# Average pooling of 8,192 rows: 15,304 neighbouring cells and 1,080 of the rest per partition, the rest loaded in two halves

## The chip, the cores and the metric

The kernel runs on one core of a Trainium2 chip. The metric is device time in microseconds of one execution; the number for a kernel is the median of several runs. A profile shows one execution from its first to its last instruction, the span; the time of a run is somewhat longer than the span.

## The reference

The input `x` is 32 x 256 x 4,096 in float32, that is 8,192 rows of 4,096 numbers (134.2 MB). Each row is cut into 256 windows of 16 neighbours, and each output cell is the mean of one window. The output is 32 x 256 x 256 in float32 (8.4 MB).

```python
for i in range(output_size):
    start = int(i * length / output_size)
    end = int((i + 1) * length / output_size)
    result[:, :, i] = np.mean(x[:, :, start:end], axis=-1)
```

Windows don't cross rows and rows lie one after the other, so in memory the whole task is 2,097,152 windows of 16 numbers in a line, each giving one cell. Where the line is cut among the 128 partitions is free.

## The kernel before, in words

The 128 partitions share the rows. The first 7,680 rows are the part called "many": partition p owns rows 60p to 60p + 59 (983,040 bytes of `x`, 15,360 cells). The other 512 rows are the part called "last": partition p owns four of them (65,536 bytes, 1,024 cells).

The loop over `t` (line 62) makes 16 tiles. In each, every partition gets four rows, 16,384 numbers: tiles 0 to 14 come from "many", tile 15 is "last". A tile lies in a buffer `xin` from a pool of two buffers (line 64), so tile t + 2 can be loaded only when the work on tile t has read its buffer for the last time. The last tile is put 32 numbers (128 bytes) into its buffer (line 65).

Per tile there are five steps.
- Line 75: SP issues the load, one DMA of 128 partitions x 65,536 bytes. At t = 1 a small memset on DVE (line 74) goes ahead of it into the same buffer, so that the load waits for it.
- Line 78: POOL adds, for the second half of the cells (512), the upper eight numbers of each window to the lower eight, in place.
- Line 83: DVE sums all 16 numbers of each window for the first half of the cells.
- Line 86: DVE sums the remaining eight numbers of each window for the second half. It waits for POOL and is the last to read the buffer.
- Line 89: ACT multiplies the 1,024 sums by 1/16, in place. The results stay in SBUF: `res_many` for tiles 0 to 14, `res_last` for tile 15.

There are three stores, all issued on SP like the loads. The one of `res_many` (7.9 MB, line 77, issued through the helper at line 58) stands in the program right behind the load of tile 15, and waits for ACT on tile 14. After the loop `res_last` is stored in two DMAs of 120 and of 8 partitions (line 95), which wait for ACT on tile 15. The program ends when all three stores have counted up the semaphore `stored` (line 100).

The order on each engine is the order of the program. The waits between engines and DMAs come from the tile framework, which tracks who writes and reads what.

Of the kernel before, what the change touches and what calls it, by code (L numbers as in the profile page):

```python
# [1 line left out]

# [4 lines left out]


@with_exitstack
def kernel(  # L10
    ctx: ExitStack,
    tc: tile.TileContext,
    x: bass.AP,
    output_size: int,
    out: bass.AP,
):

    nc = tc.nc
    F32 = mybir.dt.float32
    X = mybir.AxisListType.X

    batch, channels, length = x.shape
    ob, oc, olen = out.shape
    assert ob == batch and oc == channels and olen == output_size
    assert length % output_size == 0
    window = length // output_size  # L30
    hw = window // 2
    inv_w = 1.0 / float(window)

    P = nc.NUM_PARTITIONS
    R = 4
    rows = batch * channels
    assert rows % (P * R) == 0
    ntiles = rows // (P * R)
    many = (ntiles - 1) * R
    cells = R * output_size  # L40
    m = cells // 2
    cols = R * length

    xr = x.rearrange("b c l -> (b c) l")
    orow = out.rearrange("b c o -> (b c) o")
    x_many = xr[0 : P * many, :].rearrange("(p r) l -> p (r l)", p=P, r=many)
    o_many = orow[0 : P * many, :].rearrange("(p r) o -> p (r o)", p=P, r=many)
    x_last = xr[P * many :, :].rearrange("(p r) l -> p (r l)", p=P, r=R)
    o_last = orow[P * many :, :].rearrange("(p r) o -> p (r o)", p=P, r=R)

    res_many = nc.alloc_sbuf_tensor("res_many", [P, (ntiles - 1) * cells], F32, align_bytes=256)
    res_last = nc.alloc_sbuf_tensor("res_last", [P, cells], F32, align_bytes=256)
    inpool = ctx.enter_context(tc.tile_pool(name="inpool", bufs=2))

    stored = nc.alloc_semaphore("stored")

    def store(out, in_):
        ins = nc.sync.dma_start(out=out, in_=in_)
        tc.no_tile_sem_insts.add(ins.ins.name)
        ins.then_inc(stored, 16)  # L60

    for t in range(ntiles):
        last = t == ntiles - 1
        xbuf = inpool.tile([P, cols + 64], F32, name="xin")
        off = 32 if last else 0
        flat = xbuf[:, off : off + cols]
        xin = flat.rearrange("p (o w) -> p o w", w=window)
        if last:
            res, base, src = res_last, 0, x_last
        else:  # L70
            res, base = res_many, t * cells
            src = x_many[:, t * cols : (t + 1) * cols]
        if t == 1:
            nc.vector.memset(flat[:, 0:1536], 0.0)  # L74
        nc.sync.dma_start(out=flat, in_=src)
        if last:
            store(o_many, res_many[:, :])
        nc.gpsimd.tensor_add(  # L78
            out=xin[:, m:cells, 0:hw],
            in0=xin[:, m:cells, 0:hw],  # L80
            in1=xin[:, m:cells, hw:window],
        )
        nc.vector.reduce_sum(  # L83
            out=res[:, base : base + m], in_=xin[:, 0:m, :], axis=X
        )
        nc.vector.reduce_sum(  # L86
            out=res[:, base + m : base + cells], in_=xin[:, m:cells, 0:hw], axis=X
        )
        nc.scalar.mul(  # L89
            out=res[:, base : base + cells],  # L90
            in_=res[:, base : base + cells],
            mul=inv_w,
        )
    for lo, hi in ((0, 120), (120, P)):
        store(o_last[lo:hi, :], res_last[lo:hi, :])

    ctx.pop_all().close()
    tc.close()
    tc.compile()  # L99
    nc.sync.wait_ge(stored, 48)  # L100
    nc.sync.sem_clear(stored)


# [1 line left out]
_INS = ['x', 'output_size']  # L105
_OUTS = [((32, 256, 256), 'float32')]

_NUMBERS = {'output_size': 256}


# [26 lines left out]
```

## Time and profile before

| what | value |
|---|---|
| median of 3 runs | 333.42 us (333.3 to 333.7) |
| span of the profiled execution | 332.3 us |
| time around the span (median less span) | 1.1 us |
| DVE busy | 211.0 us (64%) |
| POOL busy | 139.7 us (42%) |
| ACT busy | 18.2 us (5%) |
| DMA packets | 2,599 with 142.61 MB, 99.4% of 16 engines' span |
| read from and written to DRAM | 134.22 MB and 8.39 MB, 429 GB/s over the span |

The profile gives busy times per engine, a picture of the span in 40 equal slices (a digit is the busy share in tenths), groups of instructions by line, the waits, and the chain of waits that ended last. The profiled execution has no other time of its own than its span; the median of the runs stands beside it. SPq is SP's queue of DMA issues. A DMA of this kernel moves one packet per partition, and 16 DMA engines share the packets; each engine ends its part of a DMA with a packet of 4 bytes that counts up a semaphore. The trace keeps a start, a duration and a size for every packet.

### The profile page before, as it was taken

What the parts mean: (1) busy time and instruction counts of PE and PEld (TensorE: products, weight loads), DVE (VectorE), ACT (ScalarE), POOL (GpSimd) and SP (SyncE); (2) the same over time, 40 slices, a digit from 0 to 9 for tenths busy, and PEclk for the clock granted to TensorE, in tenths of its full rate; (3) what the DMA queues carried; (4) which work ended last, traced back from release to release, by engine and by line L of the source; (5) the groups of instructions that cost most, each with busy time, mean ns of one, the idle gap of its engine ahead of it and who ended that gap; (6) DMA issues with size and microseconds to landing.
All of it is one profiled execution on the core that took longest, in us unless ns stands there. A gap on an engine that the chain in (4) does not pass through costs nothing.

```text
span 332.3 us, 162 instructions
## 1 busy us (share of the span) xinstructions
DVE 211.0 (64%) x33; ACT 18.2 (5%) x17; POOL 139.7 (42%) x20
## 2 busy tenths in 40 slices
DVE  1029396692939669392956939295683929578392
ACT  1000101001010100001010000101000010101001
POOL 0027091642709164370906437090633709063370
DMA  9898999989898999989898998989899898989897
GB/s 379 379 505 379 489 394 442 442 379 505 379 505 379 489 394 394 489 379 505 379 497 387 426 458 379 505 379 505 379 481 402 387 497 379 505 379 505 363 473 300
DMA packets 2599, 142.61 MB, mean 429 GB/s; under 512 B 295, under 2 KB 295, under 8 KB 423
## 3 DMA queue, kind: packets, MB, share of 16 engines
q1 hardware_dynamic: 2599, 142.61, 99.4%
HBM read 134.22 MB, written 8.39 MB: 429 GB/s over the span
## 4 chain that ended last, share of the span: by engine, by line
DMA 65%; POOL 18%; DVE 11%; POOLq 3%; issue 0%; ACT 0%
DMA xin<-in_x_dram 65%; POOL xin L78 18%; DVE res_many L86 9%; POOLq L99 3%; DVE res_last L86 1%; DVE xin L74 0%; ACT res_last L89 0%; POOLq L78 0%
## 5 line engine op out<-in xcount | busy, mean ns | idle before, releaser
L78 POOL TENSOR_TENSOR xin<-xin 128x4096 f32<-128x4096 f32 x16 | 139.5, 8717 | 181.9 <-DMA xin<-in_x_dram 181.9
L83 DVE TENSOR_REDUCE res_many<-xin 128x512 f32<-128x8192 f32 x15 | 130.3, 8686 | 105.0 <-DMA xin<-in_x_dram 105.0
L86 DVE TENSOR_REDUCE res_many<-xin 128x512 f32<-128x4096 f32 x15 | 66.3, 4420 | 2.4 <-POOL xin L78 2.3
L89 ACT ACTIVATE res_many<-res_many 128x1024 f32<-128x1024 f32 x15 | 15.8, 1056 | 289.7 <-DVE res_many L86 289.7
L83 DVE TENSOR_REDUCE res_last<-xin 128x512 f32<-128x8192 f32 x1 | 8.7, 8686 | 6.6 <-DMA xin<-in_x_dram 6.6
L86 DVE TENSOR_REDUCE res_last<-xin 128x512 f32<-128x4096 f32 x1 | 4.4, 4422 | 0.2 <-POOL xin L78 0.2
L89 ACT ACTIVATE res_last<-res_last 128x1024 f32<-128x1024 f32 x1 | 1.1, 1056 | 18.8 <-DVE res_last L86 18.8
L74 DVE MEMSET xin<- 128x1536 f32 x1 | 1.3, 1338 | 1.1 <-PEq L118 1.1
L89 ACT ACT_TABLE_LOAD x1 | 1.3, 1283 | 0.7 <-PEq L118 0.7
L118 POOL MEMSET const-float32-0.0<- 128x1 f32 x1 | 0.1, 98 | 0.2 <-issue 0.2
L118 POOL MEMSET const-bfloat16-1.0<- 128x1 bf16 x1 | 0.1, 101 | 0.0
L118 POOL MEMSET const-uint8-127<- 128x1 uint8 x1 | 0.1, 101 | 0.0
L118 POOL MEMSET const-float32-1.0<- 128x1 f32 x1 | 0.1, 98 | 0.0
## 6 DMA issues: line engine op xcount, KB each, us to landing
out_dram<-res_many SPq DMA_DIRECT2D x1, 7680.0 KB
out_dram<-res_last SPq DMA_DIRECT2D x1, 480.0 KB
xin<-in_x_dram SPq DMA_DIRECT2D x16, 25.3
out_dram<-res_last SPq DMA_DIRECT2D x1, 32.0 KB
```

The lines of the kernel that those rows point to most:

```text
L74: nc.vector.memset(flat[:, 0:1536], 0.0)
L78: nc.gpsimd.tensor_add(out=xin[:, m:cells, 0:hw], in0=xin[:, m:cells, 0:hw], in1=xin[:, m:cells, hw:window],)
L83: nc.vector.reduce_sum(out=res[:, base : base + m], in_=xin[:, 0:m, :], axis=X)
L86: nc.vector.reduce_sum(out=res[:, base + m : base + cells], in_=xin[:, m:cells, 0:hw], axis=X)
L89: nc.scalar.mul(out=res[:, base : base + cells], in_=res[:, base : base + cells], mul=inv_w,)
L99: tc.compile()
L118: nc = _bacc.Bacc("TRN2", target_bir_lowering=False, num_devices=1)
```

## The change

The line of 2,097,152 windows is cut elsewhere. "Many" now gives each partition 15,304 neighbouring cells (979,456 bytes of `x`, not a whole number of rows), and "last" gives each 1,080 (69,120 bytes). Fourteen tiles of "many" have 1,024 cells as before, the fifteenth has 968. The buffers hold 1,080 cells, and the last tile is no longer put 128 bytes into its buffer. "Last" is loaded into one buffer by two DMAs of 540 cells per partition, both issued ahead of the store of `res_many`; POOL, DVE and ACT then work on each half by itself (270 cells by the one way, 270 by the other). The stores are three as before, of 61,216 bytes per partition for `res_many` and 4,320 for `res_last`, the latter in 120 and 8 partitions.

```diff
-    R = 4
-    rows = batch * channels
-    ntiles = rows // (P * R)
-    many = (ntiles - 1) * R
-    cells = R * output_size
-    m = cells // 2
-    cols = R * length
...
-    x_many = xr[0 : P * many, :].rearrange("(p r) l -> p (r l)", p=P, r=many)
-    o_many = orow[0 : P * many, :].rearrange("(p r) o -> p (r o)", p=P, r=many)
...
+    N = 1024
+    windows = batch * channels * output_size
+    few = N + 56
+    many = windows // P - few
+    sizes = [N] * (many // N) + [many % N] * (many % N > 0)
+    cols = few * window
...
+    x_many = xf[0 : P * many * window].rearrange("(p n) -> p n", p=P)
+    o_many = of[0 : P * many].rearrange("(p n) -> p n", p=P)
+    x_last = xf[P * many * window :].rearrange("(p n) -> p n", p=P)
+    o_last = of[P * many :].rearrange("(p n) -> p n", p=P)
...
+    def pooled(flat, res):
+        n = res.shape[1]
+        m = n // 2
...
+    done = 0
+    for t, n in enumerate(sizes):
+        xbuf = inpool.tile([P, cols], F32, name="xin")
+        flat = xbuf[:, 0 : n * window]
         if t == 1:
             nc.vector.memset(flat[:, 0:1536], 0.0)
+        nc.sync.dma_start(
+            out=flat, in_=x_many[:, done * window : (done + n) * window]
         )
+        pooled(flat, res_many[:, done : done + n])
+        done += n
+
+    xbuf = inpool.tile([P, cols], F32, name="xin")
+    half = few // 2
+    halves = [(0, half), (half, few)]
+    for lo, hi in halves:
+        nc.sync.dma_start(
+            out=xbuf[:, lo * window : hi * window],
+            in_=x_last[:, lo * window : hi * window],
         )
+    store(o_many, res_many[:, :])
+    for lo, hi in halves:
+        pooled(xbuf[:, lo * window : hi * window], res_last[:, lo:hi])
     for lo, hi in ((0, 120), (120, P)):
         store(o_last[lo:hi, :], res_last[lo:hi, :])
```

`pooled` holds the add on POOL, the two reductions on DVE and the multiplication on ACT, as lines 78 to 93 did.

More of the change, by code (lines that the diff above doesn't have):

```diff
@@ L34 @@
     P = nc.NUM_PARTITIONS
-    R = 4
-    rows = batch * channels
-    assert rows % (P * R) == 0
-    ntiles = rows // (P * R)
-    many = (ntiles - 1) * R
-    cells = R * output_size
-    m = cells // 2
-    cols = R * length
-    xr = x.rearrange("b c l -> (b c) l")
-    orow = out.rearrange("b c o -> (b c) o")
-    x_many = xr[0 : P * many, :].rearrange("(p r) l -> p (r l)", p=P, r=many)
-    o_many = orow[0 : P * many, :].rearrange("(p r) o -> p (r o)", p=P, r=many)
[L48 to L52, printed above, removed]
+    N = 1024
+    windows = batch * channels * output_size
+    assert windows % P == 0
+    few = N + 56
+    many = windows // P - few
+    sizes = [N] * (many // N) + [many % N] * (many % N > 0)
+    cols = few * window
+    xf = x.rearrange("b c l -> (b c l)")
+    of = out.rearrange("b c o -> (b c o)")
+    x_many = xf[0 : P * many * window].rearrange("(p n) -> p n", p=P)
+    o_many = of[0 : P * many].rearrange("(p n) -> p n", p=P)
+    x_last = xf[P * many * window :].rearrange("(p n) -> p n", p=P)
+    o_last = of[P * many :].rearrange("(p n) -> p n", p=P)
+    res_many = nc.alloc_sbuf_tensor("res_many", [P, many], F32, align_bytes=256)
+    res_last = nc.alloc_sbuf_tensor("res_last", [P, few], F32, align_bytes=256)
     inpool = ctx.enter_context(tc.tile_pool(name="inpool", bufs=2))
@@ L60, in store @@
         ins.then_inc(stored, 16)
[L62 to L66, printed above, removed]
-        xin = flat.rearrange("p (o w) -> p o w", w=window)
[L68 to L72, printed above, removed]
+    def pooled(flat, res):
+        n = res.shape[1]
+        m = n // 2
+        xin = flat.rearrange("p (o w) -> p o w", w=window)
+        nc.gpsimd.tensor_add(
+            out=xin[:, m:n, 0:hw], in0=xin[:, m:n, 0:hw], in1=xin[:, m:n, hw:window]
+        )
+        nc.vector.reduce_sum(out=res[:, 0:m], in_=xin[:, 0:m, :], axis=X)
+        nc.vector.reduce_sum(out=res[:, m:n], in_=xin[:, m:n, 0:hw], axis=X)
+        nc.scalar.mul(out=res, in_=res, mul=inv_w)
@@ L73 @@
+    done = 0
+    for t, n in enumerate(sizes):
+        xbuf = inpool.tile([P, cols], F32, name="xin")
+        flat = xbuf[:, 0 : n * window]
         if t == 1:
             nc.vector.memset(flat[:, 0:1536], 0.0)
[L75 to L81, printed above, removed]
-        )
-        nc.vector.reduce_sum(
-            out=res[:, base : base + m], in_=xin[:, 0:m, :], axis=X
-        )
@@ L86 @@
[L86 to L93, printed above, removed]
+        nc.sync.dma_start(
+            out=flat, in_=x_many[:, done * window : (done + n) * window]
+        )
+        pooled(flat, res_many[:, done : done + n])
+        done += n
+    xbuf = inpool.tile([P, cols], F32, name="xin")
```

## The prediction

> **What bounds the kernel now.** I read the page's parts 2 and 3 first (is an engine full?), then the chain of waits (does one piece of work end last?), then the timeline of the end, then the packet records that the trace keeps for its DMA engines, one start, duration and size per packet.
>
> From the page:
> ```profile
> span 332.3 us, 162 instructions
> ...
> DVE  1029396692939669392956939295683929578392
> ...
> POOL 0027091642709164370906437090633709063370
> DMA  9898999989898999989898998989899898989897
> ...
> DMA packets 2599, 142.61 MB, mean 429 GB/s; under 512 B 295, under 2 KB 295, under 8 KB 423
> ...
> q1 hardware_dynamic: 2599, 142.61, 99.4%
> ```
> The DMA row is at 8 or 9 tenths in every slice but the last, and its packets fill 99.4% of 16 engines' span, while DVE and POOL have gaps all along. So the time is the bytes, 142.61 MB, at the engines' pace.
>
> The chain of waits seems to say something else:
> ```profile
> 273.94 8.73 POOL xin L78
> 282.67 0.02 issue
> 282.69 4.43 DVE res_many L86
> 287.12 0.02 issue
> 287.14 25.86 DMA xin<-in_x_dram
> ```
> It gives POOL 18% and DVE 11%, because it follows a load back to the reduction that freed its buffer. But the 25.86 us of that load hold a wait behind another one: load t+1 was still running when load t+2 was issued. Loads land 19.32 us apart in steady state (254.55, 273.83, 293.16 are the starts of the reductions that wait for them), so the load of 287.14 stood some 6 us in the queue. A shorter compute step would only lengthen that wait.
>
> The timeline of the end:
> ```profile
> 302.02 4.42 DVE L86 TENSOR_REDUCE res_many<-xin 128x512 f32<-128x4096 f32 x1 [0.17 <-POOL xin L78]
> 306.47 1.06 ACT L89 ACTIVATE res_many<-res_many 128x1024 f32<-128x1024 f32 x1 [18.27 <-DVE res_many L86]
> 307.55 0.35 SPq L58 DMA_DIRECT2D out_dram<-res_many  x1
> 313.02 8.69 DVE L83 TENSOR_REDUCE res_last<-xin 128x512 f32<-128x8192 f32 x1 [6.59 <-DMA xin<-in_x_dram]
> 313.13 8.72 POOL L78 TENSOR_TENSOR xin<-xin 128x4096 f32<-128x4096 f32 x1 [11.15 <-DMA xin<-in_x_dram]
> 321.88 4.42 DVE L86 TENSOR_REDUCE res_last<-xin 128x512 f32<-128x4096 f32 x1 [0.17 <-POOL xin L78]
> 326.34 1.06 ACT L89 ACTIVATE res_last<-res_last 128x1024 f32<-128x1024 f32 x1 [18.81 <-DVE res_last L86]
> 327.42 0.75 SPq L58 DMA_DIRECT2D out_dram<-res_last  x2
> ```
> The large store is issued at 307.55, before the last load has landed (313.02), and the last tile is computed while that store runs. The packet records settle whether its cover is long enough. The first packet starts at 1.76 us, 1.02 after its issue (0.74). The large store's packets start at 312.05 to 312.64, each where a load packet ended, and end at 330.2 to 330.8; the small stores' packets follow without a gap until 331.86. Chaining packets by end and next start, I find no gap over 0.06 us on any of the 16 engines. The last tile's store, issued at 327.42, could have started near 328.4 and its turn came at 330.2: the tail of compute is hidden by about 1.8 us.
>
> **A price per packet.** Median start to next start on one engine: 2,414 ns for 65,536 B, 2,264 for 61,440, 155 for 4,096. A line through the outer two is 4.4 ns + 0.03677 ns per byte; it gives 2,263 for the middle one. The 4-byte semaphore packets that end a DMA take 6. The busiest engine before: 16 loads x (8 x 2,414 + 6) = 309.09; large store 8 x 2,264 + 6 = 18.12; small stores 9 x 155 + 12 = 1.41 (120 rows on 15 engines and 8 on 8, which the 295 small packets = 17 x 16 + 15 + 8 fit); sum 328.61 us. To this come 1.76 before the first packet, 0.64 because each engine's first packet is slow (mean 3,056 against 2,418 busy), 0.35 because the last load packet of each engine, just ahead of the store, is slow too (mean 2,766), and 0.14 of small excesses between (2,201 ns over 16 engines): 331.50. Recorded: 331.86 on the last one, and 0.43 more to the end of the span at 332.29. The median of the runs, 333.42, lies 1.13 above the span; I carry that over unchanged.
>
> **The change, part by part.**
> - Loads. 14 of 65,536 B per partition: 14 x 19.318 = 270.45. One of 61,952: 8 x 2,282 + 6 = 18.26. Two halves of 34,560: 2 x (8 x 1,275 + 6) = 20.41. Stores: 61,216 B, 8 x 2,255 + 6 = 18.05; 4,320 B, 9 x 163 + 12 = 1.48. Sum 328.66, which is 0.05 us more: eight packet overheads and one semaphore packet. The bytes are the same.
> - One more DMA on SP: 0.33 us of issue (the L75 row), right after the first half's, at about 287.5. Queued behind it on SP are only the stores, the first due near 305.6. Hidden.
> - Tile 14 has 968 cells: its load ends 8 x 132 ns = 1.06 us sooner, its sum and reductions shrink by 968/1024 (8.72 to 8.24, 4.42 to 4.18), and the large store can be issued at about 292.1 + 0.1 + 8.24 + 0.1 + 4.18 + 1.0 = 305.7 instead of 307.55. Worth nothing: its packets can't start before the loads are through, near 312.1.
> - The halves take the buffer of tile 13, which is free at 287.12 as before. Tile 14's packets last until about 291.7, and packets of a DMA issued at 287.14 can start near 288.2: 3.5 us of slack (4.6 before), so the queue doesn't run dry.
> - The compute on the halves. Half 1 lands near 302.9; DVE is on tile 14 until 304.7. Half 2 lands near 313.1 and then costs 270/512 of the rows above: 4.60 on POOL, 2.33 for the second reduction, some 0.6 on ACT. The last store is issued near 320.9, not 327.42: 6.5 us earlier on paper, none of it on the path, since its packets queue behind the large store until about 330.2 either way. Were both halves to wait for the second, the reductions would sum to what they are now.
> - Layout in DRAM. A partition's rows start 979,456 B apart, not 983,040; both are multiples of 256 B. Not so in the output: 61,216 = 239 x 256 + 32 and 4,320 = 16 x 256 + 224, so seven rows of eight start off a 256 B boundary, where all started on one. No row shows a store like that. Low end: the last tile was loaded to an SBUF address 128 B off (line 65), and each engine's first seven packets of it were at 2,418 as ever: cost 0. High end: the nearest row of packets that do run slow at full load is the 0.35 us one above, 348 of 2,418 or 14%; on seven eighths of 18.05 + 1.48 us it makes 2.5 us. A gain is excluded, since stores already move a byte in the time of a load's. I take 0, the row about an odd start, and keep 2.5 for the range.
> - The other pitch can change what the slow packets cost: between -1.13 (0.64 + 0.35 + 0.14, all gone) and, by the same sum doubled, +1.13. They stand where the stream starts and turns round, not along the tiles, so I take 0.
>
> The Trainium skill, "DMA: Bandwidth & Descriptors", section on how a descriptor splits into AXI transactions, says that one which starts off a 256 B boundary pays for the bytes below its start, at most seven beats of 32 B. Its case is a read; if writes paid it too, the estimate by that page at 27.2 B/ns is 8 ns a packet, 17 packets, 0.14 us, and the sum would be +0.19 instead of +0.05; no trace here shows it.
>
> **Sum.** 333.42 + 0.05 = 333.5 us. Against the profile: last packet at 331.9, span 332.3.
>
> **The rivals.** 0.2% is 0.67 us, about what a measurement of this kernel can tell from no change.
> - A. No change (+-0.67 us, 332.8 to 334.1): the DMA engines are full from 1.76 to 331.86 and carry the same bytes. Chance 0.63.
> - B. Slower: stores that start off a boundary. Decides once a store packet takes over 36 ns more (0.62 us over 17), that is 1.7% of 2,255. For it: only the stores lose their alignment, and they stand on the path at full price. Against: a row is 61 KB, and an edge is little of that. Price up to 2.5: 335.9. Chance 0.22, with what dearer loads at the new pitch could add.
> - C. Faster: the new pitch spreads the 16 engines' first rows better, and the slow packets at both turns go: at most -1.13 + 0.05, 332.3. For it: early starters among the first packets are the slowest (2,994 to 3,538 against 2,538 for the last), as if they met somewhere. Against: some of it must be the time to fill the pipe, which no layout removes. Chance 0.15.
> - D. Faster because the tail of compute is halved. It would be worth the 6.5 us, 327.0, if the tail set the end. The 1.8 us of cover say that it doesn't; under 0.01, held within C's.
>
> Range 332.3 to 335.9: it reaches to the ends of B and C. Faster 0.15, same 0.63, slower 0.22.
>
> **What would show it.** Right: DMA still near 99.4%, the last store's issue near 321, its first packet not before 330, the chain's last waits now in DMA. Wrong in B: store packets above 2,255 ns. Wrong in C: first packets well under 3,056. Wrong in my cover: a gap in the packets ahead of the large or the last store, or before the first half.

## The result

Over 21 runs each, the changed kernel takes 334.14 us (333.97 to 334.49) and the kernel before 333.55 (333.30 to 334.05). The ratio is 1.0018, with a 95% interval from 1.0012 to 1.0025. The forecast was no change within 0.2%, and 333.5 us as its value. So the change makes the kernel slower by a little: 0.59 us, just inside the 0.67 us that were called no change, and clear of zero by its interval. The sum had given 0.05.

The page of the kernel after, the lines that answer to those shown before the change (busy tenths in 40 slices, then packets, then the DMA queue's share):
```profile
span 332.7 us, 167 instructions
...
DVE  1029396692939669392956939295693929589840
...
POOL 0027091642709064270906437090633709087320
DMA  9898999989898999989898998989899999899997
...
DMA packets 2743, 142.61 MB, mean 429 GB/s; under 512 B 311, under 2 KB 311, under 8 KB 439
...
q1 hardware_dynamic: 2743, 142.61, 99.3%
```
The bytes are the same, the packets are 144 more (128 data packets and 16 that count up a semaphore, for the second half), and the DMA engines are as full as before: 99.3% against 99.4%. DVE ends a slice earlier and POOL's last slice fell from 7 tenths to 2, while the DMA row ends as before.

The chain of waits after, its last part (start, duration, what):
```profile
287.66 15.22 DMA xin<-in_x_dram
302.88 0.02 issue
...
303.01 4.70 POOL xin L68
307.71 5.45 issue
313.16 4.73 POOLq L103
317.89 0.02 issue
317.91 2.41 DVE res_last L72
320.33 0.02 issue
320.35 0.65 ACT res_last L73
```
The chain's view ends with ACT at 321.0 us and the span with 332.7: the last 11.7 us are packets that queue, which this view doesn't follow. The forecast that its last waits would read as DMA didn't hold, because the view doesn't name that queue.

The timeline after, the same end of the kernel:
```profile
306.30 0.35 SPq L59 DMA_DIRECT2D out_dram<-res_many  x1
...
313.15 4.65 DVE L71 TENSOR_REDUCE res_last<-xin 128x270 f32<-128x4320 f32 x1 [1.05 <-DMA xin<-in_x_dram]
313.19 4.68 POOL L68 TENSOR_TENSOR xin<-xin 128x2160 f32<-128x2160 f32 x1 [5.49 <-DMA xin<-in_x_dram]
317.91 2.40 DVE L72 TENSOR_REDUCE res_last<-xin 128x270 f32<-128x2160 f32 x1
320.35 0.65 ACT L73 ACTIVATE res_last<-res_last 128x540 f32<-128x540 f32 x1 [7.57 <-DVE res_last L72]
321.03 0.88 SPq L59 DMA_DIRECT2D out_dram<-res_last  x2
```
The last stores are issued at 321.03, 6.4 us earlier than the 327.42 of before, and their first packet starts at 330.19, where it started at 330.17. The 6.4 us are gone in the queue, as the prediction had it.

What the packet records show (start to next start on one engine, medians, in ns):

```
packet            line of before    after    kernel of e8 (below)
load  65,536 B         2,414        2,417        2,414
load  61,952 B         2,282        2,286        2,282
load  34,560 B         1,275        1,279        1,275
store 61,216 B         2,255        2,260        2,255
store  4,320 B           163          168          164
```

The median packet of after is 3 to 5 ns dearer, at each size, than the line through before's packets. It isn't so from the start: by tile, the median busy time of a 65,536 B packet is 2,418 ns in tiles 1 to 3 of both kernels, and from tile 5 on 2,421 in after and 2,418 in before. The sum of the prediction with these prices is 14 x (8 x 2,417 + 6) + 8 x 2,286 + 6 + 2 x (8 x 1,279 + 6) + 8 x 2,260 + 6 + 9 x 168 + 12 = 329.17 us, not 328.66: 0.51 us more, some 0.1 too much by the cheap early tiles (4 x 8 x 3 ns). Two other terms moved as well: the slow last load packet of each engine (0.35 us before) is gone, 0.02 are left, and the first packets are slower by 0.14 (mean 3,201 ns against 3,056). That makes 0.05 + 0.51 - 0.33 + 0.14 = 0.37 us, and the last packet ends at 332.20 against 331.87, 0.33 later. The span grew by 0.45 (332.29 to 332.74) and the median of the runs by 0.59; of the difference, 0.09 is that the profiled execution of after, at 334.05, is a quick one.

### The profile page after: what moved, and what is told of

Read it like the earlier page. It is cut to its first block, busy times and chain, and to the rows that moved or that the text cites. A ratio compares the mean times of both kernels' runs of the same rounds, so it can differ in the third digit from the quotient of the medians.

```text
span 332.7 us, 167 instructions
## 1 busy us (share of the span) xinstructions
DVE 211.1 (63%) x35; ACT 18.4 (6%) x18; POOL 139.9 (42%) x21
## 2 busy tenths in 40 slices
DMA packets 2743, 142.61 MB, mean 429 GB/s; under 512 B 311, under 2 KB 311, under 8 KB 439
## 3 DMA queue, kind: packets, MB, share of 16 engines
q1 hardware_dynamic: 2743, 142.61, 99.3%
## 4 chain that ended last, share of the span: by engine, by line
DMA 62%; POOL 20%; DVE 10%; issue 2%; POOLq 1%; ACT 0%
DMA xin<-in_x_dram 62%; POOL xin L68 20%; DVE res_many L72 9%; POOLq L103 1%; DVE res_last L72 1%; DVE xin L80 0%; ACT res_last L73 0%; POOLq L68 0%
## 5 line engine op out<-in xcount | busy, mean ns | idle before, releaser
L68 POOL TENSOR_TENSOR xin<-xin 128x4096 f32<-128x4096 f32 (+2 forms) x17 | 139.7, 8216 | 177.8 <-DMA xin<-in_x_dram 177.8
L71 DVE TENSOR_REDUCE res_many<-xin 128x512 f32<-128x8192 f32 (+1 forms) x15 | 129.8, 8655 | 104.5 <-DMA xin<-in_x_dram 104.5
L72 DVE TENSOR_REDUCE res_many<-xin 128x512 f32<-128x4096 f32 (+1 forms) x15 | 66.1, 4404 | 2.4 <-POOL xin L68 2.3
L73 ACT ACTIVATE res_many<-res_many 128x1024 f32<-128x1024 f32 (+1 forms) x15 | 15.8, 1053 | 288.5 <-DVE res_many L72 288.5
L71 DVE TENSOR_REDUCE res_last<-xin 128x270 f32<-128x4320 f32 x2 | 9.3, 4648 | 1.1 <-DMA xin<-in_x_dram 1.1
L72 DVE TENSOR_REDUCE res_last<-xin 128x270 f32<-128x2160 f32 x2 | 4.8, 2398 | 0.1
L73 ACT ACTIVATE res_last<-res_last 128x540 f32<-128x540 f32 x2 | 1.3, 652 | 13.4 <-DVE res_last L72 13.4
```

The costliest lines, as they stand in the source:

```text
L68: nc.gpsimd.tensor_add(out=xin[:, m:n, 0:hw], in0=xin[:, m:n, 0:hw], in1=xin[:, m:n, hw:window])
L71: nc.vector.reduce_sum(out=res[:, 0:m], in_=xin[:, 0:m, :], axis=X)
L72: nc.vector.reduce_sum(out=res[:, m:n], in_=xin[:, m:n, 0:hw], axis=X)
L73: nc.scalar.mul(out=res, in_=res, mul=inv_w)
```

## The experiments

All times of experiments are beside the kernel before on the same chip (medians 333.48 to 333.58). Before and after have 21 runs, e9 has 4, e6 has 6, the others 11; e1, e2 and e7 have a single run each and stand in the text. "Turn" is what the packets of the last load, or of its two halves, took above the median of their size, summed per engine; "apart" is how far from one another the 16 engines end their first packet. Packet figures are of one profiled execution each.

```
kernel                      us      ratio [95% interval]      65,536 B   turn   apart  last packet
before                    333.55                              2,414 ns   0.35   0.68   331.87
after                     334.14   1.0018 [1.0012, 1.0025]    2,417      0.02   0.58   332.20
e3 cut alone, no halves   334.11   1.0020 [1.0011, 1.0029]    2,417      0.03   0.57   332.22
e4 halves alone           333.46   0.9999 [0.9990, 1.0008]    2,414      0.18   0.64   331.76
e5 no 128 B shift         333.49   1.0000 [0.9991, 1.0009]    2,414      0.41   0.65   331.72
e6 aligned cut            334.64   1.0034 [1.0022, 1.0046]    2,414      0.30   1.07   332.48
e8 after, buffers at 256  333.60   1.0001 [0.9992, 1.0009]    2,414      0.24   0.67   331.79
e9 longer tail            336.77   1.0092 [1.0077, 1.0108]    2,414      0.45   0.81   335.21
e10 first rows            334.31   1.0023 [1.0014, 1.0032]    2,414      0.10   1.29   332.57
e11 last tile at 224 B    333.44   0.9997 [0.9988, 1.0006]    2,414      0.50   0.81   332.00
e12 all tiles at 224 B    333.74   1.0007 [0.9998, 1.0016]    2,417      0.01   0.76   331.94
```

### Which part costs: the cut or the halves

The expectations weigh three theories of the dearer packets. P: a packet costs more when its row starts off a 4,096 B boundary of DRAM. B: the wider buffers in SBUF cost (this B is not the prediction's rival B). X: one execution of after was a little slow throughout.

e3, after with the last part as one:
```diff
-    halves = [(0, half), (half, few)]
+    halves = [(0, few)]
```


> After, with the last 1,080 cells loaded by one DMA and worked on as one (all of the cut in DRAM and the wide buffers, none of the halves). P and B: packets of 65,536 B stay at a mean near 2,417 start to next start. The slow last load packets (348 ns each in before, none seen in after): if the small packets of the halves took them away, they are back, and the time is some 0.35 us above after's, near 1.003 of before; if the new place or the absent 128 B shift took them away, they stay away and the time is after's, 1.002.

e4, after's code with before's cut:
```diff
-    few = N + 56
+    few = N
```


> After's code with before's cut (15,360 and 1,024 cells; buffers of 65,536 B): the halves without the new place. P: packets of 65,536 B at 2,414 again. B: also 2,414. The last store is issued some 6.5 us earlier than in before and this is worth nothing, since its packets still queue behind the large store. The slow last load packets: gone if the halves or the absent 128 B shift took them away (time about 0.3 us below before, 0.999), still there if the new place did (time of before, 1.000).

e3 has after's time and prices, e4 has before's. The halves cost and gain nothing; all of the loss comes with the cut, including what the cut does to the addresses of the buffers. In e3 a row of 69,120 B was moved as two packets of 34,560 B anyway, so it doesn't tell whether small packets remove the slow turn; e4 had a slow turn of 0.18.

The halves do what they say. The timeline of e4:
```profile
307.58 0.35 SPq L59 DMA_DIRECT2D out_dram<-res_many  x1
...
319.60 0.63 ACT L73 ACTIVATE res_last<-res_last 128x512 f32<-128x512 f32 x1 [5.96 <-DVE res_last L72]
320.26 1.03 SPq L59 DMA_DIRECT2D out_dram<-res_last  x2
```
The last stores are issued at 320.26 instead of 327.42, with a ratio of 0.9999: 7.2 us of earlier issue for nothing.

### How much the tail is covered

e9, before with the last reduction done twice:
```diff
+        if last:
+            nc.vector.reduce_sum(
+                out=res[:, base + m : base + cells], in_=xin[:, m:cells, 0:hw], axis=X
+            )
```


> The kernel before with the last tile's second reduction (line 86, 4.42 us) done twice, so that ACT and the last store come 4.44 us later (issue near 331.9 instead of 327.4). The prediction's cover of 1.8 us: the first packet of the last store starts 1.02 us after its issue, near 332.9 instead of 330.2, so the span grows by about 2.6 us, to some 335.0 (1.008). If the tail set the end already, it grows by the whole 4.4 (1.013); if the cover were larger than the delay, nothing changes.

The page of e9, its DMA row and queue, and then its timeline:
```profile
span 335.6 us, 164 instructions
...
DMA  9898989899999999998989898989899999999894
...
q1 hardware_dynamic: 2599, 142.61, 98.6%
```
```profile
326.43 4.42 DVE L90 TENSOR_REDUCE res_last<-xin 128x512 f32<-128x4096 f32 x1
330.88 1.06 ACT L93 ACTIVATE res_last<-res_last 128x1024 f32<-128x1024 f32 x1 [23.28 <-DVE res_last L90]
331.96 0.76 SPq L58 DMA_DIRECT2D out_dram<-res_last  x2
```
The issue comes 4.54 us later and the span is 3.3 us longer. The DMA row ends in a 4, where the kernel before has a 7: now the engines wait. The first packet of the last store starts at 332.82, and the large store had ended at 330.08 to 330.82. So the queue stood dry, and the cover was 4.54 less the 2.65 by which the first packet came later: 1.9 us, where the prediction had 1.8. The expected 2.6 us became 3.2 in the runs (336.77 against 333.58): packets of 4,096 B took 236 ns on average in an idle queue, not 159, which adds 9 x 77 ns = 0.7.

### Why packets are dearer: where rows start in DRAM

e1, the loads of before read from later starts:
```diff
-            src = x_many[:, t * cols : (t + 1) * cols]
+            s = (0, 0, 1024, 1024, 512, 512, 256, 256, 128, 128, 64, 64, 16, 16, 0)[t]
+            src = x_many[:, t * cols + s : (t + 1) * cols + s]
```


> The kernel before, with the loads of tiles 2 to 13 read from a later start within the same rows (so that the means are of other numbers; bytes, packets and buffers stay): tiles 2 and 3 by 4,096 B, 4 and 5 by 2,048, 6 and 7 by 1,024, 8 and 9 by 512, 10 and 11 by 256, 12 and 13 by 64. All rows of a tile then start equally far from a 4,096 B boundary of DRAM. Theory P (place: a load packet is dearer because its row starts off a 4,096 B boundary): packets of 65,536 B keep 2,414 ns start to next start in tiles 0 to 3, 14 and 15, and are 3 ns or more dearer in tiles 4 to 11, where after's mean is 2,417 with a second group 10 ns up. Theory B (the wider buffers in SBUF, 69,120 B a partition, do it): 2,414 in all tiles, since the buffers are those of before. Theory X (that one execution of after was a little slow throughout): 2,414 in all tiles. Tiles 12 and 13 (64 B off) are the case beyond what after has; P gives at least as much there as at 512.

e2, the large store in four, each with its own start:
```diff
-            store(o_many, res_many[:, :])
+            q, w = (ntiles - 1) * cells // 4, (ntiles - 1) * cells // 4 - 64
+            for j, s in enumerate((0, 8, 16, 32)):
+                store(o_many[:, j * q + s : j * q + s + w], res_many[:, j * q : j * q + w])
...
-    nc.sync.wait_ge(stored, 48)
+    nc.sync.wait_ge(stored, 96)
```


> The kernel before, with the large store cut into four stores of 3,776 cells (15,104 B) per partition that start 0, 32, 64 and 128 B off a 256 B boundary of DRAM; the sources in SBUF all start on one. It leaves 64 cells of each 3,840 unwritten. By the line through before's packets (4.4 ns and 0.03677 ns per byte) a packet takes 560 ns. P (place): about 560 in the first store and 4 to 10 ns more in those at 32 B (after's stores came out 5 ns above the line); 64 and 128 tell which boundary counts. B and X: 560 in all four. Rival B of the prediction, had it been right, asks for 1.7% (10 ns) or more.

Theory P fell in both. In e1 the median packet is 2,418 ns busy (2,414 start to next start) in every tile, whatever the start; the means of tiles 1 to 14 are 2,418 to 2,420, but for 2,430 and 2,431 in tile 11 (256 B off) and tile 12 (64 B off), where 27 and 32 of 128 packets were slow. The other tiles at these starts, 10 and 13, are at 2,418.5 and 2,419.6, and e10 below has such a patch (2,430, 26 packets) in a tile that starts where before's does. In e2 the median packet of 15,104 B takes 560 ns in all four stores. The one run of each took 333.68 and 333.39 us.

This also settles rival B of the prediction, stores that start off a 256 B boundary of DRAM: starts 32, 64 and 128 B off cost nothing in e2, and the kernel of e8 below stores to exactly after's places with packets on the line (2,255 and 164).

### Why packets are dearer: where rows start in SBUF

After's `res_last` is 4,320 B long, and the buffers `xin` follow it in SBUF without padding: by the addresses that the program gives them they start at 82,400 and 151,520, both 224 B behind a multiple of 256. Before's start at 82,176 and 147,968, both on one. The new theory, A, was that this is what costs. P2, what was left of P, was that rows of one DMA that differ in their place in DRAM cost.

e7, the tiles of before put into their buffers at eight different starts:
```diff
-        off = 32 if last else 0
+        off = (t // 2) * 8
```


> The kernel before, with tiles put into their buffers at 0, 32, 64, 96, 128, 160, 192 and 224 B, two tiles each in this order (results unchanged). DRAM side as before. Theory A: load packets of 65,536 B at 2,414 ns start to next start up to 128 B, and 3 to 10 ns dearer in tiles 10 to 15 (160 to 224 B), most at 224, as in after (2,417, some 2,424). P2: 2,414 in all tiles, since only the rows' places in DRAM count.

Mean busy time of a 65,536 B packet in e7, by the tile's start in its buffer (first of each pair, then the second; tile 0 holds the slow first packets, tile 15 the turn):

```
start      0 B    32     64     96    128    160    192    224
tile 2k     -   2419.7 2418.7 2419.8 2421.6 2422.2 2421.7 2422.6
2k + 1   2419.5 2418.9 2418.5 2420.5 2421.8 2421.4 2421.9 2426.3
```
From 128 B on, packets are dearer by 2 to 4 ns, and by 1 or 2 at 96 B, a little sooner than A had it. But the start grows with the tile's number here, and e12 below shows that the number counts as well, so e7 can't tell from which start on it costs. A start at 128 B is among the dear ones, and yet the last tile of before, at 128 B, had its first seven packets at 2,418. The one run took 333.85 us.

e8, after with the buffers moved:
```diff
-    res_last = nc.alloc_sbuf_tensor("res_last", [P, few], F32, align_bytes=256)
+    res_last = nc.alloc_sbuf_tensor("res_last", [P, few + 8], F32, align_bytes=256)[:, 0:few]
```


> After with res_last allocated 8 cells longer and nothing else changed: the buffers that follow it in SBUF then start on a 256 B boundary instead of 224 B behind one. Theory A: load packets back at 2,414 ns; 14 x 8 x 3 ns + 8 x 4 + 16 x 4 = 0.43 us come back, the stores' 0.06 to 0.1 don't, so about 333.7 where after has 334.1 (1.0005 of before). P2: packets stay at 2,417 and the time is after's (1.002).

All prices are back on the line (the table of packets above), the stores' too, although their addresses in SBUF and DRAM are after's. The time is 333.60, with a ratio of 1.0001 [0.9992, 1.0009]: of the 0.59 us, 0.09 are left, with 32 bytes of padding. P2 falls, since the rows' places in DRAM are after's. The page of e8:
```profile
span 332.3 us, 167 instructions
...
q1 hardware_dynamic: 2743, 142.61, 99.3%
```
The span is that of before with after's 2,743 packets.

e12, the same start in before:
```diff
-        off = 32 if last else 0
+        off = 56
```


> The kernel before with every tile 224 B into its buffer (line 65: 56 numbers in all tiles), as after's buffers lie; the cut in DRAM, the packets' sizes and the stores are those of before. Theory A (the buffers' start in SBUF is what after pays for): load packets at 2,417 ns or more start to next start, about 0.5 us above before, 1.0016. If theory A is also all there is to the dearer stores of after, packets of 61,440 B are some 5 ns above 2,264 here, though their own addresses have not changed; and the slow last load packets are absent, as in the three kernels that had most tiles there. Rival: the cost in after came from the buffers' start together with the new cut; then the time is that of before.

The median load packet goes to 2,417 as in after, and the slow turn vanishes. But the time rises by 0.26 us only, an interval from 0.9998 to 1.0016 that holds both no change and most of A's 0.5; and the packets of 61,440 B stay at 2,264, so why after's stores were dearer is not explained by it. So the buffers' start is needed for after's loss, as e8 shows; what it costs by itself e12 does not tell from nothing.

The packet records show one thing more. Of the 128 packets of a tile, so many took exactly 2,418 ns busy, the median of before:

```
tile                       3     4     5     8    11
before                   102    99   107   120   127
e8 after, at 256         102   102   110   124   126
after, all at 224        105    62    27     5    12
e12, all at 224           91    71    35    43    31
e7, start of the tile    107   111   113    19    17
                        32 B    64    64   128   160
```
In after and e12 every tile starts at the same place, and yet the first tiles are as cheap as before's. The dearer price sets in during the stream, around tile 4 or 5, and in e12 part of the packets falls back for a while. So it is not a price per packet that the address sets; in these traces the stream goes over to a dearer pattern only where the buffers start off the boundary. What makes it go over is not known.

### The slow turn from loads to stores

e5, before without the 128 B:
```diff
-        off = 32 if last else 0
+        off = 0
```


> The kernel before with the last tile at the start of its buffer (line 65: 0 in place of 32 numbers). For the slow last load packets ahead of the large store (excess 348 ns each in before, none in after, some 160 ns in the halves alone): if the 128 B shift makes them, they go, last packet near 331.5 us and the time about 0.3 us below before (0.999). If they belong to the turn from loads to stores whatever the address, they stay and the time is that of before (1.000).

e11, before with the last tile alone at 224 B:
```diff
-        off = 32 if last else 0
+        off = 56 if last else 0
```


> The kernel before with the last tile 224 B into its buffer instead of 128 (line 65: 56 numbers in place of 32). The slow last load packets ahead of the large store (excess 0.35 us per engine) were absent in the three kernels whose last load lies 224 B behind a 256 B boundary, and there with 0 and mostly there with 128. If that address takes them away, the excess is below 0.1 us, the eight packets of the last load cost 4 ns more each (0.03 us), and the time is about 0.3 us below before, 0.999: faster than both kernels. If the slowness has only been spread over all of after's packets (the same loss in other records), the excess comes back or shows up elsewhere, and the time is that of before.

Neither takes the slow turn away (0.41 and 0.50 us), and neither changes the time (1.0000 and 0.9997). e11 was the try at a kernel faster than both, and it isn't one. The turn is quick in the four kernels in which many tiles before it start late in a 256 B block (after, e3, e7, e12). That fits the other reading named for e11: one loss, put down at the turn in one kernel and spread over the packets in the other. The mean over engines from the end of the first packet to the end of the last load is 307.23 us in before and 307.19 in e12, although e12's median load packet is 3 ns dearer from tile 5 on, which is 0.26 us for 88. This is weak support: the same figure runs from 306.96 (e2) to 307.28 (e1) in kernels whose median packet costs the same. The quick turns of e2 (0.04) and e10 (0.10), where the median load was no dearer, don't fit the reading, and it was not tested by itself.

### The cut with everything aligned

e6, after with rows that start on 4,096 B in DRAM and buffers on 256 B:
```diff
-    few = N + 56
+    few = N + 64
```


> After with 8 more cells in the last part: 15,296 and 1,088 cells, so that rows in DRAM lie 978,944 B (239 x 4,096) and in the output 61,184 B (239 x 256) apart, and both buffers start on a 256 B boundary of SBUF (after's start 224 B behind one). The halves stay. Theory A (a packet is dearer when its row starts late in a 256 B block, in SBUF or DRAM): load packets of 65,536 B back at 2,414 ns, stores on before's line (61,184 B: 2,254), together 0.5 us below after, 1.000 of before. Theory P2 (rows of one DMA that differ in their place in DRAM) says the same here. If packets stay at 2,417, neither holds and the cut itself or the width of the buffers costs.

Packets are back at 2,414 (stores of 61,184 B at 2,254), and yet this is the slowest cut: 334.64 us, 1.0034. Its engines end the first packet 1.07 us apart and the loads 1.12 apart. e10 takes only the place of the first rows into before:
```diff
+        if t == 0:
+            pitch = 15296 * window
+            flat_x = x.rearrange("b c l -> (b c l)")
+            src = flat_x[0 : P * pitch].rearrange("(p n) -> p n", p=P)[:, 0:cols]
```


> The kernel before with tile 0 alone read from rows that lie 978,944 B apart (the pitch of the aligned cut) instead of 983,040, so that its means are of other numbers; everything else as before. The aligned cut had all its packets at before's prices and was still 1.003 of before; in its profile the 16 engines ended their first packets 1.07 us apart (0.68 in before) and were 1.12 us apart at the end of the loads. Theory S (where the first rows lie sets how far the engines start apart, and they stay so to the end): about 1.07 us apart here too, and 334.2 to 334.6 us, 1.002 to 1.003. Rival (the aligned cut loses at its end, in its halves of 34,816 B): spread and time of before, 1.000.

The rows of one tile of sixteen cost 0.73 us (334.31 against 333.58), and the engines are 1.29 us apart from the first packet on. Kernels that read the first tile where before does have 0.37 (e2) to 0.81, so this is outside their scatter. One engine ended its loads at 313.20 where the others had ended by 312.37; the mean over the engines, 312.10, is earlier than before's 312.23. The page of e10:
```profile
span 332.9 us, 162 instructions
...
q1 hardware_dynamic: 2599, 142.61, 99.1%
```
Same packets and bytes as before, at the same median price, and 99.1% instead of 99.4: a late engine leaves the others idle at the end. By the medians this is 0.73 of e6's 1.13 us, if e6's rows cost it what they cost e10. The other 0.4 stay open, and the trace of e6 can't show them: its execution took 334.15, the least of six (up to 334.84), only 0.64 above before.

## Why the prediction was right, and where it was wrong

- The bound held. Full DMA engines with the same bytes gave the same time to 0.2%, though at the edge of it: the interval of the ratio ends at 1.0025. That it stayed inside was in part luck. For e6, a cut 8 cells per partition further, the same reasoning gives no change, and it costs 1.13 us.
- The halves held point by point: no gain from the earlier issue (e4), a cover of 1.9 us against 1.8 (e9; its packets came 0.86 us after the issue, not 1.02), no gap over 0.02 us from the first load to the end of the large store, the large store's issue at 306.30 (305.7 forecast) and the last store's at 321.03 (320.9 forecast).
- The price per packet held for size: with the buffers on a 256 B boundary, e8's five sizes, four of them absent before, lie within 1 ns of the line.
- The step that failed is the item on the layout and with it the sum, "0.05 us more". It looked for the price of an odd start in DRAM alone. There it is 0 for every start tried (e1, e2). The start that costs is that of the buffers in SBUF, which the diff doesn't show: it follows from the 4,320 B of `res_last` ahead of them. The row cited for "cost 0", the last tile at 128 B, was the right kind of row, and too short: one tile at the end, whose eighth packets were slow anyway, where the dearer price of after took four tiles to set in. In size, the terms are about 0.4 to 0.5 us of dearer packets, 0.33 back at the turn and 0.14 at the start in the profile; 0.59 in the runs, of which e8 leaves 0.09.
- Rival B had the right sign and the wrong mechanism. Its own mark, store packets above 2,255 ns, did appear (2,260), but at 5 ns, far from the 36 that it needed, and it goes away in e8 with the stores' places unchanged. Its 2.5 us don't exist. Rival C's idea that the rows' place moves the slow first packets is shown, in the other direction: after's pitch left the start as it was (0.58 against 0.68 apart), and another pitch made it worse (e6, e10).
- The Trainium skill's rule in "DMA: Bandwidth & Descriptors" (how a descriptor splits into AXI transactions) was weighed for the stores' DRAM side. e2 and e8 show no such cost on that side: 560 ns at every start in e2, and 2,255 in e8, the price by size alone.
- Three small slips in the working change nothing. The 1.13 us between span and time mix two executions; where both are on record for one, it is 1.26 to 1.36. 36 of 2,255 ns is 1.6%, not 1.7. And the early starters' first packets take from 2,898 ns up, not from 2,994.

What stays open: how the 0.59 us divide between the start of the buffers alone (0.26 in e12, within an interval that touches zero) and its working together with the new cut, what makes the stream go over to the dearer price, and whether the slow turn and the dearer packets are one loss.

## What to carry to other kernels

Where the DMA queue is full to the end, ask of a faster tail only whether its last store was already queued in time; 6 us earlier was worth nothing here, and 4.5 us later cost 3.2. After changing the size of any tensor in SBUF, look where the buffers behind it now start: 32 bytes of padding took 0.5 of this change's 0.59 us away. And look how far apart the engines end their first packet: in e10 the place of the first tile's rows alone cost 0.73 us, more than the whole change.

## What the hardware showed beside this

- A packet's price is linear in its bytes from 4,096 to 65,536: 4.4 ns and 0.03677 ns per byte on one engine, 27.2 GB/s, with all 16 engines moving (before, and e8 within 1 ns).
- With buffers in SBUF that start 224 B behind a 256 B boundary, packets of 65,536 B went from 2,418 ns busy to 2,421 around tile 4 or 5 and, in the main, stayed there (after, e12); with buffers on the boundary they stayed at 2,418 (before, e8). Reads that started 64 to 2,048 B off a 4,096 B boundary of DRAM did nothing to the median (e1).
- Engines that start apart stay apart: 0.68 us at the first packet and 0.59 at the end of the loads in before, 1.29 and 1.35 in e10. By their code, the two kernels differ in the pitch of the first tile's rows alone.
- Packets that reach an idle queue are dearer than in a full one: 236 ns on average for 4,096 B in e9, 159 in before.
